# Softmax shares through the output bank, and weight pieces ordered behind matmuls, in a two-layer decoder kernel

## The chip, the cores and the metric

The kernel runs on one core of a Trainium2 chip. The metric is the device time of one execution in microseconds (us). A program for this core has five engines that run side by side, each with its own queue of instructions: TensorE (PE in the profile, with its weight loads as PEld), VectorE (DVE), ScalarE (ACT), GpSimd (POOL) and SyncE (SP, which here only issues DMAs).

## What is computed

The reference is a decoder of two layers on 512 tokens of width 1024, in fp32. Layer 0 is sparse attention beside memory attention and a squared-ReLU MLP. Then keys and values are computed once from the residual stream, and layer 1 reads them:

```python
k_s, v_s = jnp.split(rmsnorm(x, kv_norm) @ w_kv_shared, 2, axis=-1)
...
q, q_mem = jnp.split(h @ b_w_in[i], [B_Q], axis=-1)
o_main = dilated_attention(q, k_shared, v_shared, b_q_norm[i])
o_mem = memory_attention(q_mem, mem_kv, mem_q_norm[layer], mem_k_norm[layer])
x = x + jnp.concatenate([o_main, o_mem], axis=-1) @ b_w_out[i]
...
x = x + squared_relu_mlp(rmsnorm(x, mlp_norm[layer]), w_up[layer], w_down[layer])
```

The dilated attention of layer 1 has 8 heads and three groups of keys (window 128 at every position, 512 at every fourth, 2048 at every sixteenth). Each group has its own softmax, and the three outputs are added with weights that are a softmax over the groups' log-sums. The kernel calls these weights shares.

## The kernel before

Every matmul on fp32 data is made of three matmuls on split operands: a value is kept as a high part and the remainder (`mm3`, L234 to L239; lines 237, 238 and 239 are the three matmuls). A weight tile is loaded by SP into a staging buffer `st` (three buffers, `wdma`), and split into a tile `w` (four buffers) by one ACT and one DVE instruction.

Where the input of a projection went through a norm, the norm's gain is multiplied into the weights as they are split. `wload` then makes one piece per 128 rows of the contraction: `part` (L250) issues ACT L253 for the high part and DVE L254 for the remainder. Seven projections of layer B are of this kind: K and V (width 512), q of the four head pairs (width 384) and q of the memory attention (width 256). Each has eight contraction steps, so eight pieces.

`proj` (L277) runs a projection over four blocks of 128 tokens; a step is three matmuls for one of the eight pieces. During the first block (at steps 0, 2 and 4 with two steps per tile, at step 0 with four) it loads weight tiles so that two are ahead, and issues all pieces of a tile at once. The matmuls of the q projections go to two accumulator banks `s_acc`. A finished block is evacuated by `normf` (ACT L474, DVE L476 to L483) and DVE L1431, and some steps later its heads are transposed on PE (L677) into a bank of `s_pt` and copied out by ACT (L683, L1439).

PSUM has eight banks: two `s_acc`, three `s_ps` (scores), two `s_pt` (transposes) and one `s_po` (outputs of P times V).

Layer B runs K's projection, then q's of pair 0 and V's, then the attention of four head pairs. `attend` issues the attention as items, and between items takes steps from a list of other work: q of pairs 1 to 3 with their keys, q and keys of the memory attention, and parts of the output projection. An item's `front` makes scores, their maximum (DVE L1521) and the exponentials (ACT L1531); its `back`, one item later, transposes the probabilities (L1551, L1560) and, at the end of a group, multiplies by V (`close0` L1573 and `close1` L1586, in `s_po`).

The shares of a pair are a side chain, one step per tick:

- `turned_b` takes the first group's maxima and sums, transposes them (L1602), copies them to a row with the tokens in another order (DVE L1604), transposes back (L1608) and copies (DVE L1610).
- `shares_b` makes the shares from both groups' maxima and sums in small DVE operations (L1618 to L1630), splits them, transposes them (L1637), copies the rows (DVE L1641), and spreads them over the 64 columns of each head by a matmul each for the two groups: L1645, copied by ACT L1647, and L1649, multiplied into the first output by DVE L1650. `join_b` does the same for the second output and adds.

All five bank uses of this chain are in `s_pt`.

The text of the program is not the order on the engines. The program is built with

```python
with tile.TileContext(nc, schedule_with_timeline_sim=True) as tc:
```

which plans each engine's queue from simulated times: among the instructions whose inputs are there in the simulation, the one earlier in the text goes first. On the chip the queues run in that order, and semaphores hold an instruction until its inputs and buffers are ready.

Of the kernel before, what the change touches and what calls it, by code (L numbers as in the profile page):

```python
# [11 lines left out]
AF = mybir.ActivationFunctionType  # L12
ALU = mybir.AluOpType
AX = mybir.AxisListType

P = 128
D = 1024
S = 512
NB = 4
KT = 8  # L20
# [14 lines left out]
def bcast(ap, dim, n):  # L35

    a = [list(x) for x in ap.ap]
    a.insert(dim, [0, n])
    return bass.AP(tensor=ap.tensor, offset=ap.offset, ap=a)
# [13 lines left out]

WK = 0.4
DELAY = 5

NY, NZ = 1, 1
END, WAIT = object(), object()
# [106 lines left out]
class K:  # L165
# [46 lines left out]
        self.nc.sync.dma_start(st, src)  # L212
        return st

    def wload(self, src, lo="v", gains=None):

        st = self.wdma(src)
        w = self.t("w", [P, 2, src.shape[-1]], F32R)
        if gains is None:
            self.wsplit(w, st, lo)  # L220
            return w
        n = src.shape[-1] // gains.shape[1]
        for j in range(gains.shape[1]):
            c = slice(j * n, (j + 1) * n)
            self.part(w[:, :, c], st[:, c], gains[:, j : j + 1])
        return w

    def wsplit(self, w, st, lo):
# [5 lines left out]
    def mm3(self, ps, lh, rh, start, stop, again=False):  # L234

        mm = self.nc.tensor.matmul
        mm(ps, lh[0], rh[0], start=start, stop=False, skip_group_check=again)  # L237
        mm(ps, lh[0], rh[1], start=False, stop=False, skip_group_check=again)  # L238
        mm(ps, lh[1], rh[0], start=False, stop=stop, skip_group_check=again)  # L239

    def gcol(self, gname):

# [7 lines left out]
    def part(self, dst, src, g):  # L250

        nc = self.nc
        nc.scalar.activation(dst[:, 0], src, AF.Copy, scale=g)  # L253
        nc.vector.scalar_tensor_tensor(  # L254
            out=dst[:, 1], in0=src, scalar=g, in1=dst[:, 0], op0=ALU.mult, op1=ALU.subtract
        )

    def xg(self, x, gname):

# [17 lines left out]
    def proj(self, xg, wsrc, n, evac, blocks=NB, per=2, stat=None, banks=None, pool=None, lo="v", fine=False, hook=None, order=None, gain=None):  # L277


        ws = []  # L280
        if not stat:
            stat = lambda k, b: [xg[k][:, h, b * P : (b + 1) * P] for h in (0, 1)]

        def step(ps, k, b):
            w = ws[k // per]
            o = (k % per) * n
            self.mm3(ps, stat(k, b), [w[:, h, o : o + n] for h in (0, 1)], k == 0, k == KT - 1)

        late = []

        def tick(n=DELAY):
            for x in list(late):
                x[0] += 1
                if x[0] >= n:
                    late.remove(x)
                    x[1]()

        def out(b, ps):
            f = evac(b, ps)
            if f:  # L300
                late.append([0, f])

        if banks:
            banks = [self.ps(p, [P, n]) for p in banks]
            for k in range(KT):
                if hook:
                    hook(k)
                o = (k % per) * n
                if k % per == 0 and fine:
                    st = self.staged.pop(0) if self.staged else self.wdma(wsrc[k // per])  # L310
                    ws.append(self.t("w", [P, 2, per * n], F32R))
                elif k % per == 0:
                    ws.append(self.wload(wsrc[k // per], lo[len(ws) % len(lo)]))
                w = ws[-1]
                if fine:
                    self.wsplit(w[:, :, o : o + n], st[:, o : o + n], lo[k % len(lo)])
                for b in range(blocks):
                    self.mm3(banks[b], stat(k, b), [w[:, h, o : o + n] for h in (0, 1)], k == 0, k == KT - 1)
                yield
            for b in range(blocks):  # L320
                out(b, banks[b])
                yield
                tick(1)
        nw = KT // per
        order = order or range(blocks)
        for b in [] if banks else order:
            ps = None
            for k in range(KT):
                if b == order[0]:
                    while len(ws) < min(nw, k // per + 2):  # L330
                        i = len(ws) * per
                        gs = self.gcol(gain)[:, i : i + per] if gain else None
                        ws.append(self.wload(wsrc[len(ws)], lo[len(ws) % len(lo)], gs))
                if ps is None:
                    ps = self.ps(pool[b] if isinstance(pool, list) else pool or self.pacc, [P, n])
                step(ps, k, b)
                yield
                tick()
            out(b, ps)
            yield  # L340
        while late:
            tick()
            yield
# [1134 lines left out]
    def attn_b(self, sp, q4, kv, oT, side):  # L1478

        nc = self.nc  # L1480
        st0 = self.t("stt", [P, NB, 4])
        st1 = self.t("stt", [P, NB, 4])
        t0, t1 = {}, {}

        def front(s, w, ih):

            kp4 = kv[0]
            st = (st0, st1)[w]
            sizes = [P, 256] if w == 0 and ih == 0 else [256, 256]
            Sp = self.ps(self.pS, [P, sum(sizes)])  # L1490
            o = 0
            for ii in range(2):
                i, n = 2 * ih + ii, sizes[ii]
                blk = slice(i * P, (i + 1) * P)
                if w == 0:
                    for hl in (0, 1):
                        k = kp4[hl][:, s, (i + 1) * 32 - n // 4 :]
                        k = bass.AP(
                            tensor=k.tensor, offset=k.offset, ap=[list(k.ap[0]), [32, n // P], [P, 4], [1, 32]]
                        )  # L1500
                        nc.tensor.matmul(
                            Sp[:, o : o + n].rearrange("p (j r u) -> p j r u", r=4, u=32), q4[0][:, s, blk], k,
                            start=ii == 0 and hl == 0, stop=False,
                        )
                    nc.tensor.matmul(Sp[:, o : o + n], self.idb, self.bm0[:, 256 - n :], start=False, stop=ii == 1)
                else:
                    for g in range(2):
                        for hl in (0, 1):
                            nc.tensor.matmul(
                                Sp[:, o + g * P : o + g * P + P], q4[1 + g][:, s, blk], kp4[hl][:, s, blk],  # L1510
                                start=ii == 0 and g == 0 and hl == 0, stop=False,
# [25 lines left out]
                pg = p.rearrange("p (r g k) -> p r g k", r=2, g=2)  # L1537
                nc.gpsimd.tensor_tensor(out=pg[:, :, 0, :], in0=pg[:, :, 0, :], in1=pg[:, :, 1, :], op=ALU.add)
            if s == 1 and ih == 1:
                side.add(self.shares_b(st1, s0, acc) if w else self.turned_b(st0, s0))  # L1540
            return p

        def back(s, w, ih, p):
# [18 lines left out]
            if s == 1 and ih == 1:  # L1562
                close1()

        acc, s0 = [], []

        def close0():
            vn = kv[1]
# [25 lines left out]
        order = [(s, w, ih) for w in range(2) for s in range(2) for ih in range(2)]  # L1594
        return [Item(front, back, a, sp, sp or None) for a in order]

    def turned_b(self, st0, res):

        nc = self.nc
        pt = self.ps(self.pT, [4, S])  # L1600
        for b in range(NB):
            nc.tensor.transpose(pt[:, b * P : (b + 1) * P], st0[:, b, :], self.idf)  # L1602
        row = self.t("p2", [4, S])
        nc.vector.tensor_copy(row.rearrange("p (r u) -> p r u", r=4), self.perm(pt))  # L1604
        yield
        pt = self.ps(self.pT, [P, NB, 4])
        for r_ in range(NB):
            nc.tensor.transpose(pt[:, r_, :], row[:, r_ * P : (r_ + 1) * P], self.idf[0:4, 0:4])  # L1608
        s0 = self.t("stt", [P, NB, 4])
        nc.vector.tensor_copy(s0, pt)  # L1610
        res.append(s0)

    def shares_b(self, st1, s0, acc):

        nc = self.nc
        s0 = s0[0]
        m = self.t("nb", [P, NB, 2])
        nc.vector.tensor_tensor(out=m, in0=s0[:, :, 0:2], in1=st1[:, :, 0:2], op=ALU.min)  # L1618
        ee = self.t("nb", [P, 2, NB, 2])
        nc.vector.tensor_tensor(out=ee[:, 0], in0=m, in1=s0[:, :, 0:2], op=ALU.subtract)  # L1620
        nc.vector.tensor_tensor(out=ee[:, 1], in0=m, in1=st1[:, :, 0:2], op=ALU.subtract)
        nc.scalar.activation(ee, ee, AF.Exp)
        z = self.t("nb", [P, 2, NB, 2])
        nc.vector.tensor_tensor(out=z[:, 0], in0=ee[:, 0], in1=s0[:, :, 2:4], op=ALU.mult)
        nc.vector.tensor_tensor(out=z[:, 1], in0=ee[:, 1], in1=st1[:, :, 2:4], op=ALU.mult)
        nc.vector.tensor_tensor(out=m, in0=z[:, 0], in1=z[:, 1], op=ALU.add)
        nc.vector.reciprocal(out=m, in_=m)
        cc = self.t("nb", [P, NB, 2, 2])
        for w_ in range(2):
            nc.vector.tensor_tensor(out=cc[:, :, w_, :], in0=ee[:, w_], in1=m, op=ALU.mult)  # L1630
        ch = self.t("nb", [P, NB, 2, 4], F32R)
        self.split(ch.rearrange("p r t c -> p t r c"), cc.rearrange("p r w s -> p r (w s)"), "v")
        for _ in range(NY):
            yield
        pt = self.ps(self.pT, [8, S])
        for r_ in range(NB):
            nc.tensor.transpose(  # L1637
                pt[:, r_ * P : (r_ + 1) * P].bitcast(F32R), ch[:, r_].rearrange("p t c -> p (t c)"), self.idr
            )
        rows = self.t("p2", [8, S], F32R)  # L1640
        nc.vector.tensor_copy(rows, pt)  # L1641
        for _ in range(NZ):
            yield
        pc = self.ps(self.pT, [P, S])
        nc.tensor.matmul(pc, self.sel[:, 1, :], rows, start=True, stop=True)  # L1645
        cb = self.t("p2", [P, S])
        nc.scalar.activation(cb, pc, AF.Copy)  # L1647
        pc = self.ps(self.pT, [P, S])
        nc.tensor.matmul(pc, self.sel[:, 0, :], rows, start=True, stop=True)  # L1649
        nc.vector.tensor_tensor(out=acc[0], in0=acc[0], in1=pc, op=ALU.mult)  # L1650
        acc.append(cb)
# [135 lines left out]
```

## Time and profile before

| | |
|---|---|
| median of 3 runs | 1300.62 us (1298.31 to 1304.62) |
| the profiled execution's own time | 1302.66 us |
| its span, first to last instruction | 1300.6 us |
| mean granted TensorE clock | 0.990 |

In a profile's timeline a line has the start and the length in us, the engine, the line of the kernel, the operation, the output and inputs by tile name, shapes, a count, and in brackets the idle time of the engine before it and what ended that. An entry with a count is several instructions merged. In the waits, a line names the waiting engine and line, what it waited for, and the total us, the number of waits and the longest. Starts are counted from the span's start. Layer B before its MLP lies between about 675 and 960 us; the first weight piece of K's projection (ACT L253) starts at 677.2 us, and the last one, of the memory attention's q, at 842.7 us.

### The profile page before, as it was taken

Reading aid. Unit: us, or ns where it says so; the run is one execution under the profiler, and the core shown is the slowest. Engines: PE = TensorE matmul, PEld = TensorE weight load, DVE = VectorE, ACT = ScalarE, POOL = GpSimd, SP = SyncE. Lnnn points to the kernel's source line nnn. Section 1 sums busy time; section 2 is a strip of 40 time slices with the busy share of each in tenths; the row PEclk is TensorE's granted clock in tenths of the full one; section 3 lists DMA queues with packets and bytes.
Section 4 is the critical chain, followed back from the end, with each engine's and each line's share of the span. In section 5 each row is a group of like instructions: output and inputs, shape, how many; then the busy total and the mean of one; then the engine's idle time right before and its main releaser. Section 6 shows DMA issues by size and latency. Waiting matters only on the chain.

```text
span 1300.6 us, 18592 instructions
## 1 busy us (share of the span) xinstructions
PE 1252.5 (96%) x6425; PEld 1017.7 (78%) x6425; DVE 987.0 (76%) x1687; ACT 765.6 (59%) x1763; POOL 540.1 (42%) x569
## 2 busy tenths in 40 slices
PE   8998999999999999999999998899899999999998
PEld 6776776677787888888878897787678788888886
DVE  5978777764679678696799678776658968779678
ACT  5757667773555464554566576776666545455452
POOL 3766565532164241441425946442316424144241
PEclk9999999999999999999999999999899999999999
DMA  8222211023423425335254242002242442623423
GB/s 304 96 73 100 66 36 55 18 66 124 139 86 120 140 97 170 121 96 164 82 149 146 78 129 75 25 26 76 86 135 83 137 138 82 194 98 119 145 93 114
DMA packets 52686, 139.11 MB, mean 107 GB/s; under 512 B 5776, under 2 KB 14992, under 8 KB 52592
## 3 DMA queue, kind: packets, MB, share of 16 engines
q1 hardware_dynamic: 51376, 134.66, 32.9%
q0 software_dynamic: 640, 2.21, 0.5%
q8 instruction: 51, 0.84, 0.2%
q10 hardware_dynamic: 576, 1.05, 0.2%
q14 instruction: 43, 0.35, 0.1%
HBM read 132.66 MB, written 5.24 MB: 106 GB/s over the span
## 4 chain that ended last, share of the span: by engine, by line
PE 59%; DVE 24%; ACT 10%; DMA 3%; issue 2%; POOL 2%; ACTq 0%; POOLq 0%; DVEq 0%
PE s_ps L238 10%; PE s_ps L239 10%; PE s_ps L237 10%; DVE s_w L232 7%; PE s_acc L237 4%; PE s_acc L238 4%; PE s_acc L239 4%; DVE s_p L1114 2%; PE s_po L1055 2%; PE s_pt L238 2%; PE s_pt L239 2%; PE s_pt L237 2%; ACT s_w L230 2%; DVE s_w L254 2%; DVE s_qk L275 2%
## 5 line engine op out<-in xcount | busy, mean ns | idle before, releaser
L232 DVE TENSOR_TENSOR s_w<-s_st,s_w 128x1024 fp32r<-128x1024 f32 (+4 forms) x155 | 183.9, 1188 | 138.3 <-ACT s_w L230 138.0
L230 ACT ACTIVATE s_w<-s_st 128x1024 fp32r<-128x1024 f32 (+4 forms) x182 | 166.0, 917 | 137.9 <-PE s_pt L239 39.5
L237 PE MATMUL s_ps<-s_act,s_w 128*128 128x512 f32 x592 | 231.8, 393 | 3.2 <-ACT s_act L272 1.4
L238 PE MATMUL s_ps<-s_act,s_w 128*128 128x512 f32 x592 | 231.0, 390 | 0.0
L239 PE MATMUL s_ps<-s_act,s_w 128*128 128x512 f32 x592 | 230.9, 391 | 0.0
L1100 POOL TENSOR_TENSOR s_x<-s_x,s_st 128x512 f32<-128x512 f32 x64 | 106.0, 1679 | 91.0 <-DVE s_w L232 91.0
L237 PEld LDWEIGHTS s_ps<-s_act,s_w 128*128 128x128 f32 x592 | 110.9, 188 | 28.0 <-ACT s_act L272 3.2
L239 PEld LDWEIGHTS s_ps<-s_act,s_w 128*128 128x128 f32 x592 | 111.2, 188 | 22.9
L238 PEld LDWEIGHTS s_ps<-s_act,s_w 128*128 128x128 f32 x592 | 111.2, 188 | 22.8 <-DVE s_act L275 0.4
L237 PE MATMUL s_acc<-s_w,s_act 128*128 128x512 f32 (+2 forms) x304 | 112.0, 374 | 9.8 <-ACT s_w L230 6.0
L1100 POOL TENSOR_TENSOR s_x<-s_qki,s_st 128x512 f32<-128x512 f32 x16 | 25.5, 1596 | 216.2 <-DMA s_st<-in_w_db_dram 196.6
L238 PE MATMUL s_acc<-s_w,s_act 128*128 128x512 f32 (+2 forms) x304 | 111.6, 368 | 1.4 <-DVE s_w L232 0.9
L239 PE MATMUL s_acc<-s_w,s_act 128*128 128x512 f32 (+2 forms) x304 | 109.4, 364 | 0.0
L652 POOL TENSOR_SCALAR s_p<-s_p,s_cr 128x256 f32<-128x256 f32 (+3 forms) x128 | 70.9, 568 | 68.3 <-DVE s_cr L1018 20.2
L232 DVE TENSOR_TENSOR s_w<-s_x,s_w 128x512 fp32r<-128x512 f32 x96 | 89.3, 971 | 4.9 <-ACT s_w L230 4.9
L275 DVE TENSOR_TENSOR s_qk<-s_p,s_qk 128x256 fp32r<-128x256 f32 (+1 forms) x96 | 83.9, 886 | 2.8 <-ACT s_qk L272 1.8
L230 ACT ACTIVATE s_w<-s_x 128x512 fp32r<-128x512 f32 x96 | 56.8, 624 | 41.0 <-POOL s_x L1100 41.0
L232 POOL TENSOR_TENSOR s_w<-s_st,s_w 128x512 fp32r<-128x512 f32 (+4 forms) x27 | 39.0, 1443 | 87.0 <-ACT s_w L230 84.3
L272 ACT ACTIVATE s_qk<-s_p 128x256 fp32r<-128x256 f32 (+1 forms) x96 | 47.0, 489 | 45.4 <-DVE s_p L1228 43.2
L237 PEld LDWEIGHTS s_acc<-s_w,s_act 128*128 128x128 f32 x304 | 58.7, 195 | 16.6 <-ACT s_w L230 6.2
L238 PEld LDWEIGHTS s_acc<-s_w,s_act 128*128 128x128 f32 x304 | 59.3, 195 | 7.8 <-DVE s_w L232 1.8
L1222 ACT ACTIVATE s_p<-s_ps 128x512 f32<-128x512 f32 x64 | 37.8, 591 | 46.1 <-PE s_ps L239 43.8
(357 smaller groups left out, 3223.6 us busy)
## 6 DMA issues: line engine op xcount, KB each, us to landing
s_st<-in_w_db_dram SPq DMA_DIRECT2D x80, 512.0 KB, 3.6
s_st<-in_w_up_dram SPq DMA_DIRECT2D x64, 512.0 KB, 3.8
s_st<-in_w_bq_dram SPq DMA_DIRECT2D x16, 384.0 KB, 3.3
s_st<-in_w_ag_dram SPq DMA_DIRECT2D x11, 512.0 KB, 4.3
s_act<-in_w_c_dram SPq DMA_DIRECT2D x8, 512.0 KB, 5.4
s_st<-in_w_mem_dram SPq DMA_DIRECT2D x8, 512.0 KB, 3.6
s_st<-in_w_ao_dram SPq DMA_DIRECT2D x16, 256.0 KB, 2.7
s_tq<-in_w_db_dram SPq DMA_DIRECT2D x16, 256.0 KB, 3.1
```

The lines of the kernel that those rows point to most:

```text
L230: nc.scalar.activation(w[:, 0], st, AF.Copy)
L232: self.low = e.tensor_tensor(out=w[:, 1], in0=st, in1=w[:, 0], op=ALU.subtract)
L237: mm(ps, lh[0], rh[0], start=start, stop=False, skip_group_check=again)
L238: mm(ps, lh[0], rh[1], start=False, stop=False, skip_group_check=again)
L239: mm(ps, lh[1], rh[0], start=False, stop=stop, skip_group_check=again)
L254: nc.vector.scalar_tensor_tensor(out=dst[:, 1], in0=src, scalar=g, in1=dst[:, 0], op0=ALU.mult, op1=ALU.subtract)
L272: nc.scalar.activation(dst[:, 0], src, AF.Copy)
L275: nc.vector.tensor_tensor(out=dst[:, 1], in0=src, in1=dst[:, 0], op=ALU.subtract)
L652: self.nc.gpsimd.tensor_scalar(out=p, in0=p, scalar1=c, scalar2=1.0, op0=ALU.mult, op1=ALU.mult)
L1055: nc.tensor.matmul(O[x * 64 : x * 64 + 64, q0 + o : q0 + 256], v[:, j, br, :], st[x][br][:, j, o:256], start=half == 0 and br == 1 and j = ...
L1100: self.nc.gpsimd.tensor_tensor(out=o, in0=x, in1=b[:, i * 512 : (i + 1) * 512], op=ALU.add)
L1222: nc.scalar.activation(u, ps, AF.Relu)
```

## The change

Two things are changed.

The shares' chain takes its five banks per pair from `s_po` (pool `pO`, one bank) in place of `s_pt` (pool `pT`, two banks). Its statistics of both groups now lie in one tile, so that three pairs of small DVE operations become one operation each.

In `proj`, pieces with a gain are not issued as soon as their tile is loaded. They are kept in a list, and at step k of the first block as many are issued as bring the number made to k + 3. From step 1 on each of the two instructions of a piece gets an edge to the last matmul issued so far. The edge has the class `NoSync`: it orders the planning and adds no semaphore.

```diff
+AHEAD = 3
+DEPC, DEPR = mybir.DependencyClass.NoSync, mybir.DependencyReason.DATA
...
-    def wload(self, src, lo="v", gains=None):
+    def wload(self, src, lo="v", gains=None, late=None):
...
-            self.part(w[:, :, c], st[:, c], gains[:, j : j + 1])
+            f = lambda c=c, j=j: self.part(w[:, :, c], st[:, c], gains[:, j : j + 1])
+            if late is None:
+                f()
+            else:
+                late.append(f)
...
-        mm(ps, lh[1], rh[0], start=False, stop=stop, skip_group_check=again)
+        self.last = mm(ps, lh[1], rh[0], start=False, stop=stop, skip_group_check=again)
...
-                        ws.append(self.wload(wsrc[len(ws)], lo[len(ws) % len(lo)], gs))
+                        ws.append(self.wload(wsrc[len(ws)], lo[len(ws) % len(lo)], gs, parts))
+                    while parts and made < min(KT, k + AHEAD):
+                        f = parts.pop(0)
+                        for x in f():
+                            if k:
+                                self.tc.add_manual_dep(x.ins, self.last.ins.name, mybir.DependencyInfo(DEPC, DEPR), reason="late split")
+                        made += 1
...
-        st1 = self.t("stt", [P, NB, 4])
+        sb = self.t("stt", [P, 2, NB, 4])
+        st1 = sb[:, 1]
...
-        pt = self.ps(self.pT, [4, S])
+        pt = self.ps(self.pO, [4, S])
...
-        pt = self.ps(self.pT, [P, NB, 4])
+        pt = self.ps(self.pO, [P, NB, 4])
...
-        nc.vector.tensor_tensor(out=ee[:, 0], in0=m, in1=s0[:, :, 0:2], op=ALU.subtract)
-        nc.vector.tensor_tensor(out=ee[:, 1], in0=m, in1=st1[:, :, 0:2], op=ALU.subtract)
+        tt(ee, bcast(m, 1, 2), sb[:, :, :, 0:2], ALU.subtract)
...
-        nc.vector.tensor_tensor(out=z[:, 0], in0=ee[:, 0], in1=s0[:, :, 2:4], op=ALU.mult)
-        nc.vector.tensor_tensor(out=z[:, 1], in0=ee[:, 1], in1=st1[:, :, 2:4], op=ALU.mult)
+        tt(z, ee, sb[:, :, :, 2:4], ALU.mult)
...
-        for w_ in range(2):
-            nc.vector.tensor_tensor(out=cc[:, :, w_, :], in0=ee[:, w_], in1=m, op=ALU.mult)
+        tt(cc.rearrange("p r w s -> p w r s"), ee, bcast(m, 1, 2), ALU.mult)
...
-        pt = self.ps(self.pT, [8, S])
+        pt = self.ps(self.pO, [8, S])
...
-        pc = self.ps(self.pT, [P, S])
+        pc = self.ps(self.pO, [P, S])
...
-        pc = self.ps(self.pT, [P, S])
+        pc = self.ps(self.pO, [P, S])
```

More of the change, by code (lines that the diff above doesn't have):

```diff
@@ L252, in part @@
         nc = self.nc
[L253 to L256, printed above, removed]
+        return [
+            nc.scalar.activation(dst[:, 0], src, AF.Copy, scale=g),
+            nc.vector.scalar_tensor_tensor(
+                out=dst[:, 1], in0=src, scalar=g, in1=dst[:, 0], op0=ALU.mult, op1=ALU.subtract
+            ),
+        ]
     def xg(self, x, gname):
@@ L323, in proj @@
                 tick(1)
-        nw = KT // per
+        nw, parts, made = KT // per, [], 0
         order = order or range(blocks)
@@ L1539, in front @@
             if s == 1 and ih == 1:
-                side.add(self.shares_b(st1, s0, acc) if w else self.turned_b(st0, s0))
+                side.add(self.shares_b(sb, acc) if w else self.turned_b(st0, sb[:, 0]))
             return p
@@ L1563, in back @@
                 close1()
-        acc, s0 = [], []
+        acc = []
         def close0():
@@ L1595, in attn_b, with turned_b @@
         return [Item(front, back, a, sp, sp or None) for a in order]
-    def turned_b(self, st0, res):
+    def turned_b(self, st0, s0):
         nc = self.nc
-        pt = self.ps(self.pT, [4, S])
+        pt = self.ps(self.pO, [4, S])
         for b in range(NB):
@@ L1605, in turned_b, with shares_b @@
         yield
-        pt = self.ps(self.pT, [P, NB, 4])
+        pt = self.ps(self.pO, [P, NB, 4])
         for r_ in range(NB):
             nc.tensor.transpose(pt[:, r_, :], row[:, r_ * P : (r_ + 1) * P], self.idf[0:4, 0:4])
-        s0 = self.t("stt", [P, NB, 4])
         nc.vector.tensor_copy(s0, pt)
-        res.append(s0)
-    def shares_b(self, st1, s0, acc):
+    def shares_b(self, sb, acc):
         nc = self.nc
-        s0 = s0[0]
+        tt = lambda o, x, y, op: nc.vector.tensor_tensor(out=o, in0=x, in1=y, op=op)
         m = self.t("nb", [P, NB, 2])
-        nc.vector.tensor_tensor(out=m, in0=s0[:, :, 0:2], in1=st1[:, :, 0:2], op=ALU.min)
+        tt(m, sb[:, 0, :, 0:2], sb[:, 1, :, 0:2], ALU.min)
         ee = self.t("nb", [P, 2, NB, 2])
-        nc.vector.tensor_tensor(out=ee[:, 0], in0=m, in1=s0[:, :, 0:2], op=ALU.subtract)
-        nc.vector.tensor_tensor(out=ee[:, 1], in0=m, in1=st1[:, :, 0:2], op=ALU.subtract)
+        tt(ee, bcast(m, 1, 2), sb[:, :, :, 0:2], ALU.subtract)
         nc.scalar.activation(ee, ee, AF.Exp)
         z = self.t("nb", [P, 2, NB, 2])
-        nc.vector.tensor_tensor(out=z[:, 0], in0=ee[:, 0], in1=s0[:, :, 2:4], op=ALU.mult)
-        nc.vector.tensor_tensor(out=z[:, 1], in0=ee[:, 1], in1=st1[:, :, 2:4], op=ALU.mult)
-        nc.vector.tensor_tensor(out=m, in0=z[:, 0], in1=z[:, 1], op=ALU.add)
+        tt(z, ee, sb[:, :, :, 2:4], ALU.mult)
+        tt(m, z[:, 0], z[:, 1], ALU.add)
         nc.vector.reciprocal(out=m, in_=m)
         cc = self.t("nb", [P, NB, 2, 2])
-        for w_ in range(2):
-            nc.vector.tensor_tensor(out=cc[:, :, w_, :], in0=ee[:, w_], in1=m, op=ALU.mult)
+        tt(cc.rearrange("p r w s -> p w r s"), ee, bcast(m, 1, 2), ALU.mult)
         ch = self.t("nb", [P, NB, 2, 4], F32R)
```

## The prediction

> **What bounds the kernel now.** The page comes first, for the engine that sets the time.
>
> ```profile
> PE 1252.5 (96%) x6425; PEld 1017.7 (78%) x6425; DVE 987.0 (76%) x1687; ACT 765.6 (59%) x1763; POOL 540.1 (42%) x569
> ```
>
> TensorE is busy for 1252.5 of 1300.6 us, so idle PE time in the whole program is 48.1 us, and no edit that leaves the matmuls as they are can win more than that plus what a slow clock costs. The change touches only layer B before its MLP, so the next view is the busy time by stretch there, chosen in pairs: a stretch at half clock, and the one just ahead of it. The columns are the stretch, its length, busy us (instructions) of PE, PEld, DVE, ACT and POOL, the granted clock, the DMA share, GB/s.
>
> ```profile
> 799.80:806.40 6.60, 4.66 (x30) 3.99 (x29) 6.57 (x12) 6.10 (x17) 3.38 (x4) 1.00 0.49 132
> 806.50:809.90 3.40, 3.40 (x13) 3.40 (x12) 3.40 (x5) 2.21 (x7) 3.19 (x4) 0.50 0.40 161
> 843.90:847.30 3.40, 1.36 (x13) 1.20 (x13) 2.99 (x9) 2.35 (x9) 1.55 (x2) 1.00 0.66 180
> 847.40:850.80 3.40, 3.40 (x19) 3.40 (x18) 3.37 (x8) 2.17 (x8) 3.17 (x5) 0.51 0.16 46
> 915.00:919.00 4.00, 2.60 (x15) 1.61 (x13) 3.02 (x6) 1.37 (x5) 0.45 (x1) 1.00 0.57 144
> 919.20:929.30 10.10, 9.79 (x40) 7.46 (x40) 5.64 (x11) 6.86 (x23) 2.50 (x5) 0.50 0.30 92
> ```
>
> Three times PE is poorly filled (4.66 of 6.60, 1.36 of 3.40, 2.60 of 4.00 us) and then runs at half clock though it is full. Matmul work done at 0.50 takes twice as long, so the half-clock stretches cost about 1.7, 1.7 and 5.0 us. Next, what PE waited for in that stage, from the waits of PE between 650 and 940 us (total, times, longest).
>
> ```profile
> PE s_pt L677 <- DVE s_p L1641: 1.5, 1, 1.5
> PE s_pt L1637 <- ACT s_qk L1439: 1.4, 1, 1.4
> PE s_pt L1645 <- ACT s_qk L635: 1.4, 1, 1.4
> ...
> PE s_acc L237 <- DVE s_tq L1431: 1.1, 1, 1.1
> ...
> PE s_acc L238 <- DVE s_w L254: 0.5, 1, 0.5
> ```
>
> The first three are waits for a bank of the transposes' pool, s_pt: the shares (L1637, L1645) wait for one, or q's transposes (L677) wait for the bank that the shares hold until L1641 has copied it. The fourth is a projection that waits for its accumulator. Only the last is a matmul that waits for a weight piece. Then the timelines show why these were late. PE, then ACT, then DVE:
>
> ```profile
> 843.52 0.41 PE L1637 MATMUL s_pt<-idr,s_nb 128*8 128x128 f32 x4 [1.38 <-ACT s_qk L1439]
> 845.38 0.70 PE L677 MATMUL s_pt<-idr,s_qki 128*128 128x128 f32 x6 [1.46 <-DVE s_p L1641]
> ```
>
> ```profile
> 841.51 1.69 ACT L253 ACTIVATE s_w<-s_st,gv 128x256 fp32r<-128x256 f32 x4
> 843.10 0.36 ACT L1439 ACTIVATE s_qk<-s_pt 128x256 fp32r<-128x256 f32 x1
> ```
>
> ```profile
> 841.19 3.54 DVE L254 SCALAR_TENSOR_TENSOR s_w<-s_st,gv,s_w 128x256 fp32r<-128x256 f32 x8
> 844.66 0.67 DVE L1641 CAST s_p<-s_pt 8x512 fp32r<-8x512 f32 x1
> ```
>
> L1439, which would empty a bank, stands on ACT behind four weight pieces; L1641, which would empty the other, stands on DVE behind all eight. The accumulator's wait has the same form, here on DVE and on PE:
>
> ```profile
> 799.77 4.54 DVE L254 SCALAR_TENSOR_TENSOR s_w<-s_st,gv,s_w 128x384 fp32r<-128x384 f32 x6
> ...
> 804.81 0.56 DVE L1431 TENSOR_TENSOR s_tq<-s_acc,gr 128x384 f32<-128x384 f32 x1
> ```
>
> ```profile
> 805.42 0.44 PE L237 MATMUL s_acc<-s_w,s_act 128*128 128x384 f32 x1 [1.05 <-DVE s_tq L1431]
> ```
>
> Six pieces run in a block, the evacuation L1431 comes after them, and PE starts 0.05 us after it ends. So two things meet in this stage: the shares take banks that transposes need, and pieces for the next projection, made in one block, hold up the evacuations that free banks.
>
> **Part 1, the shares through the O bank.** Five bank uses per head pair leave s_pt (two banks) for s_po (one, which until now holds the two P times V outputs). Out of the sum go the three s_pt waits: 1.5 + 1.4 + 1.4 = 4.3 us. New is that in one bank each use must be emptied before the next. Three of these waits are there already as data (rows copied before the next transposes, and so on). Two are new: the second share product L1649 waits for the copy L1647 of the first, and the second P times V, L1586, waits for the product L1650. PE, ACT and DVE of one pair:
>
> ```profile
> 816.09 0.49 PE L1645 MATMUL s_pt<-s_p,s_ab 8*128 8x512 f32 x1
> ...
> 818.27 0.49 PE L1649 MATMUL s_pt<-s_p,s_ab 8*128 8x512 f32 x1
> ...
> 820.84 0.55 PE L1586 MATMUL s_po<-s_pt,s_x 128*64 128x128 f32 x6 [0.31 <-ACT s_pt L660]
> ```
>
> ```profile
> 816.61 0.60 ACT L1647 ACTIVATE s_p<-s_pt 128x512 f32<-128x512 f32 x1 [0.70 <-PE s_pt L1645]
> ```
>
> ```profile
> 818.80 0.69 DVE L1650 TENSOR_TENSOR s_raw<-s_raw,s_pt 128x512 f32<-128x512 f32 x1 [0.76 <-PE s_pt L1649]
> ```
>
> The copy ends at 817.21, 1.06 us before L1649 begins; the product ends at 819.49, 1.35 us before L1586 begins. Both new waits would have been over here, so I cost them at nothing; matmuls of the projection and the next pair's scores lie between them and are the cover. Without cover each pair pays the copy and the product, 0.60 + 0.69, or 5.2 us over four pairs. Behind a waiting L1649 or L1586 in PE's queue stand exactly those matmuls.
>
> **Part 2, the shares' smaller form.** Three of the small DVE operations per pair go, twelve in all, of about this size (from the groups of lines):
>
> ```profile
> L1630 DVE TENSOR_TENSOR s_nb<-s_nb,s_nb 128x8 f32<-128x8 f32 x8 | 2.3, 325 | 0.1
> ```
>
> That is some 12 x 0.325 = 3.9 us of DVE time. Each joined one is twice as long in elements, so the gain may be near nothing. On PE's path I count 0: by the rows above, the shares' end is not what L1586 waits for.
>
> **Part 3, the pieces.** Seven projections (K, V, four of q, mem q) make eight pieces each, one ACT and one DVE instruction per piece. The first three stay free; piece j of the other five is queued behind the last matmul of step j - 3 (or of other work, if that stands later in the text). No instruction is added. Moved past them on ACT and DVE are the evacuations (L1439, L1641, L1431), and that takes out the 1.1 us of the accumulator, and with the shares' banks gone from s_pt also what would be late next: with L1637 elsewhere, L677 would still have waited for L1439 behind the four ACT pieces. The loads on SP keep their order, but a staging buffer comes free when its last piece is made, so the next load, and the loads behind it in SP's queue, may start later. Five pieces of 0.83 us (row below) bound that at 4.1 us per projection; the load is issued a tile ahead of its use, which covers it, and I count 0.
>
> Against that, pieces come closer to their use. Their pace on DVE, from the groups by shape between 700 and 930 us (count, then busy us and mean ns):
>
> ```profile
> L254 DVE SCALAR_TENSOR_TENSOR s_w<-s_st,gv,s_w 128x384 fp32r<-128x384 f32 x32 | 25.0, 827 | 4.2 <-ACT s_w L253 4.2
> ...
> L254 DVE SCALAR_TENSOR_TENSOR s_w<-s_st,gv,s_w 128x512 fp32r<-128x512 f32 x8 | 9.0, 1174 | 0.0
> ```
>
> And the pace at which a block uses them, two starts nine matmuls, or three steps, apart:
>
> ```profile
> 799.18 0.33 PE L237 MATMUL s_acc<-s_w,s_act 128*128 128x384 f32 x1
> ...
> 800.74 0.33 PE L237 MATMUL s_acc<-s_w,s_act 128*128 128x384 f32 x1
> ```
>
> A step of width 384 takes 1.56 / 3 = 0.52 us, so by width 0.69 for 512 and 0.35 for 256; a piece of 256 is by width 0.55. PE can outrun DVE by 0.31, 0.48 or 0.20 us per ordered piece. Five pieces: 4 x 5 x 0.31 + 2 x 5 x 0.48 + 5 x 0.20 = 12.0 us if nothing else fills PE, and 0 if scores and transposes do. The nearest row is V's first block, whose pieces are the slow ones of 1.174 us and are used almost as made: it shows a PE wait of 0.5 us. I take that for V and the three q projections inside attention: 2.0 us.
>
> **The clock.** The two half-clock stretches at 806.5 and 847.4 follow the very stretches whose waits go, so I take off 1.7 + 1.7. Ahead of the third, one of two waits goes (the 1.4 of L1645); I take one 3.4 us part of its three as gone, 1.7. The Trainium skill, "TensorE: Matmul & The Clock Gate", in "Why this matters for your kernels", asks only that PE not be idle for more than about 3 us between bursts. The longest of the waits quoted is 1.46 us and the clock halved all the same, so the measurement decides against that rule; by it this term would be zero, and the time that of the first rival.
>
> **The sum.** Waits gone: 4.3 + 1.1 = 5.4. Clock: 5.1. Back again: 2.0 for pieces, and 1.4 because I expect one of the three bank waits to be replaced by another. -5.4 - 5.1 + 2.0 + 1.4 = -7.1 us. The profiled execution took 1302.66 us (span 1300.6), so it would take 1295.6; it lies 2.0 above the median of the runs, 1300.62, inside their spread of 1298.31 to 1304.62. On the median the forecast is 1293.5.
>
> **Rivals.**
>
> *The clock stays.* What comes before a slow stretch is not only waits but transposes (L677, L1462, L1637), and those stay. The same page, in "Part 4: PE-mode transpose", says that transposes do not count as busy in the way matmuls do. If they are what halves the clock, only the waits go: -5.4 + 3.4 = -2.0, or 1298.6, no change. For it: the 1.36 of 3.40 before 847.4 is almost all transposes. Against it: the waits are there in all three run-ups too, and no row here shows the one without the other. Chance 0.15.
>
> *The order does not hold the pieces apart.* The edges shape the queues when they are planned; no semaphore is added. If the planner issues the matmuls early, or ACT and DVE fall behind it, pieces run in a block as before. Then the accumulator's 1.1 and L1439's wait stay, and only about 1.5 us of bank waits goes: 1299.1, no change. Chance 0.10.
>
> *The first blocks starve, and it is slower.* DVE is busy for 6.57 of 6.60 us before 806.4, so late pieces compete with the evacuations that they used to delay. If nothing fills PE, the 12.0 us are paid, and each of the four first blocks inside attention is a poorly filled stretch that brings its own 1.7 us at half clock, 6.8. With the forecast's gains kept: 12.0 + 6.8 - 5.4 - 5.1 = +8.3, or 1308.9. It becomes slower by over 0.5% when more than about 10 of the 12.0 us stay uncovered. For it: just-in-time work gives up what was made early. Against it: 0.5 us of such waits where the pieces are slowest. Chance 0.20.
>
> **How the numbers follow.** Half a per cent, 6.5 us, is about what a measurement of this kernel can tell from no change: faster is below 1294.1, slower above 1307.1. The forecast has 0.55, its own range is 1287 (all 8.4 us of slow clock gone, nothing back: -13.8) to 1298, and the point lies just inside faster; I put 0.43 of it there and 0.12 in no change. No change gets 0.12 + 0.15 + 0.10 = 0.37, slower 0.20, faster 0.43. The range for 8 in 10 leaves out half of the slow case above 1309 and the best tenth below 1285.
>
> **What would show it.** Right: up to about 660 us the two traces agree; L1637, L1645 and L1649 write s_po; the three s_pt waits are gone; L254 comes in runs of one to three; fewer stretches at 0.50 between 800 and 930 us; DVE has twelve fewer instructions. Wrong: PE waits for L253 or L254 of more than 2 us, waits of s_po matmuls for L1647 or L1650, or new half-clock stretches at the start of a projection.

## The result, and the profile after

The changed kernel takes 1287.72 us (median of 6 runs, 1286.79 to 1289.21) where the kernel before takes 1300.51 (6 runs): a ratio of 0.9903, 95% interval 0.9887 to 0.9918, so 12.8 us less. The profiled execution took 1286.79 us, with a span of 1285.0 and a mean granted clock of 0.999. Later, beside the last experiments, the same kernel gave 0.9895 (0.9878 to 0.9911).

Lines of the code have moved: the three matmuls are L243 to L245 in the kernel after, a piece is ACT L260 and DVE L261, the evacuation L1431 is L1445, the copies L1439 are L1453, q's transposes L677 are L691, and the shares' L1637, L1645 and L1649 are L1647, L1655 and L1659.

The first view cuts the program at marks that both kernels have: the first piece of K's projection, the last piece of the memory attention's q, and the last gain-scaled activation of the MLP behind layer B. The columns are those of the prediction's stretches. The kernel before, then the kernel after:

```profile
677.20:746.00 68.80, 67.06 (x335) 57.52 (x334) 56.65 (x118) 41.51 (x115) 45.49 (x61) 1.00 0.39 127
746.00:842.70 96.70, 91.14 (x609) 83.20 (x607) 73.35 (x145) 69.88 (x217) 50.42 (x62) 0.98 0.25 74
842.70:962.80 120.10, 108.97 (x687) 86.08 (x688) 81.93 (x180) 85.00 (x256) 35.68 (x52) 0.94 0.25 76
```

```profile
674.70:744.00 69.30, 68.91 (x342) 58.79 (x341) 57.46 (x118) 41.32 (x117) 45.96 (x63) 1.00 0.40 126
744.00:839.40 95.40, 92.36 (x634) 84.49 (x634) 74.36 (x148) 72.42 (x230) 54.66 (x65) 1.00 0.26 76
839.40:947.40 108.00, 100.51 (x663) 79.92 (x662) 76.83 (x164) 79.88 (x243) 34.02 (x48) 0.98 0.28 84
```

Layer B takes 272.7 us in place of 285.6, 12.9 us less, as much as the whole change of the medians. Most of it (12.1) lies in the last stretch. PE's idle time, length less busy time, falls from 18.4 to 10.9 us (-7.5), and its busy time from 267.2 to 261.8 (-5.4) although it does the same matmuls: that part is the clock, 0.94 and 0.98 before in the later stretches, 0.98 and 1.00 after. All runs together say the same. A run's time multiplied by its mean granted clock is an estimate of what it would take without half clock, since PE is nearly always busy in the half-clock stretches of the kernel before (3.40 of 3.40 and 9.79 of 10.10 us). The kernel before has 57 runs beside the experiments and the kernel after has 10 in all: by their means this estimate falls from 1289.7 to 1281.9 us (-7.8), and the rest of the time, the clock's part, from 10.9 to 5.5 us (-5.4). The MLP behind takes 337.8 and 337.6 us. Ahead of layer B the profiled execution of after gains 2.5 us (677.2 to 674.7). There the queues of PE, DVE, ACT and POOL have the same order in both traces. The trace of before has 10.2 us at half clock there and that of after none, and such stretches come and go between runs.

The waits of PE between 670 and 960 us come to 17.7 us before and 9.5 after. The first of them after:

```profile
PE s_acc L244 <- DVE s_w L261: 3.7, 5, 1.7
PE s_acc L243 <- DVE s_x L1108: 1.5, 1, 1.5
PE s_ps L601 <- ACT s_p L660: 1.1, 1, 1.1
```

No wait for a share's bank is left, and none of an accumulator for L1445. The longest sum is now matmuls that wait for a weight piece, 3.7 us in five waits, where there was one of 0.5. Two of them stand in the first block of the memory attention's q:

```profile
838.07 0.39 PE L244 MATMUL s_acc<-s_w,s_act 128*128 128x256 f32 x1 [0.63 <-DVE s_w L261]
...
841.87 0.58 PE L244 MATMUL s_acc<-s_w,s_act 128*128 128x256 f32 x1 [1.70 <-DVE s_w L261]
```

```profile
838.30:841.70 3.40, 1.75 (x12) 1.31 (x11) 3.20 (x7) 3.30 (x11) 2.97 (x4) 1.00 0.44 115
841.70:845.10 3.40, 3.23 (x16) 3.24 (x17) 3.40 (x8) 1.95 (x6) 2.59 (x3) 0.50 0.29 78
```

This is the one half-clock stretch that layer B has left in this trace, and it has the form of the three before: PE filled for 1.75 of 3.40 us, then half clock. In sum layer B spent 17.0 us at half clock before and 3.4 after.

### The profile page after: what moved, and what is told of

Same layout as the page of the kernel before. It is cut to its first block, busy times and chain, and to the rows that moved or that the text cites. A ratio compares the mean times of both kernels' runs of the same rounds, so it can differ in the third digit from the quotient of the medians.

```text
span 1285.0 us, 18569 instructions
## 1 busy us (share of the span) xinstructions
PE 1241.8 (97%) x6425; PEld 1009.8 (79%) x6425; DVE 981.1 (76%) x1675; ACT 762.4 (59%) x1763; POOL 543.0 (42%) x569
## 4 chain that ended last, share of the span: by engine, by line
PE 66%; DVE 20%; ACT 7%; DMA 3%; issue 2%; POOL 1%; ACTq 0%; DVEq 0%; POOLq 0%
PE s_ps L244 11%; PE s_ps L245 10%; PE s_ps L243 10%; DVE s_w L238 7%; PE s_acc L244 5%; PE s_acc L243 5%; PE s_acc L245 5%; PE s_pt L244 3%; PE s_pt L245 3%; PE s_pt L243 3%; DVE s_p L1128 2%; PE s_po L1069 2%; ACT s_w L236 2%; DVE s_qk L283 2%; PE s_acc L834 1%
## 5 line engine op out<-in xcount | busy, mean ns | idle before, releaser
L243 PE MATMUL s_ps<-s_act,s_w 128*128 128x512 f32 x592 | 231.7, 393 | 1.9 <-ACT s_act L280 1.4
L245 PE MATMUL s_ps<-s_act,s_w 128*128 128x512 f32 x592 | 230.8, 390 | 0.0
L243 PEld LDWEIGHTS s_ps<-s_act,s_w 128*128 128x128 f32 x592 | 111.0, 188 | 26.8 <-ACT s_act L280 3.2
L245 PEld LDWEIGHTS s_ps<-s_act,s_w 128*128 128x128 f32 x592 | 111.2, 188 | 22.9
L243 PE MATMUL s_acc<-s_w,s_act 128*128 128x512 f32 (+2 forms) x304 | 110.6, 369 | 6.9 <-ACT s_w L236 6.1
L245 PE MATMUL s_acc<-s_w,s_act 128*128 128x512 f32 (+2 forms) x304 | 108.2, 360 | 0.0
L243 PEld LDWEIGHTS s_acc<-s_w,s_act 128*128 128x128 f32 x304 | 58.0, 192 | 13.6 <-ACT s_w L236 6.3
L244 PEld LDWEIGHTS s_acc<-s_w,s_act 128*128 128x128 f32 x304 | 58.3, 192 | 12.8 <-DVE s_w L261 6.2
```

Of the source, the lines that this page charges most:

```text
L245: self.last = mm(ps, lh[1], rh[0], start=False, stop=stop, skip_group_check=again)
```

## The experiments

Three explanations stood against each other. A: shares and pieces each remove waits of their own, and both count. B: only the pieces matter, since the banks were late because evacuations stood behind pieces. C: any new order of the queues moves the time by some microseconds, whatever it is meant for. All ratios are to the kernel before, run on the same chip (medians there 1299.81 to 1301.05 us), with 95% intervals.

**The shares alone.** The whole change of the shares; pieces are issued at once.

```diff
-ws.append(self.wload(wsrc[len(ws)], lo[len(ws) % len(lo)], gs, parts))
+ws.append(self.wload(wsrc[len(ws)], lo[len(ws) % len(lo)], gs))
```

> The shares through the O bank with their smaller form; all weight pieces of a tile issued at once, as in the kernel before. Theory A (the two parts work on two different waits and add up): the three bank waits of the shares go, and with them most of the half-clock stretches at 847 and 919 us, so about half of the gain: 1300.5 - 6, near 1294 to 1295; waits of an accumulator for L1431's counterpart behind a block of pieces stay. Theory B (only the pieces matter, since the banks were late because of the evacuations queued behind pieces): within 2 us of 1300.5. Theory C (any new order of the queues gives some gain or loss of this size): no relation to the parts; this and the kernel with the pieces alone need not add up to 12.8.

Measured: 1292.18 us (9 runs, 1286.76 to 1296.4), ratio 0.9934 (0.9913 to 0.9956). B is out: more than half of the gain is there without touching a piece. What the pieces were to remove is still in its waits, and larger than before the change:

```profile
PE s_acc L243 <- DVE s_tq L1445: 2.7, 2, 1.9
PE s_acc L244 <- DVE s_w L261: 1.5, 4, 0.5
```

**The pieces alone.** `attn_b`, `turned_b` and `shares_b` as in the kernel before, all else as after.

> The pieces held back and ordered behind matmuls; the shares as in the kernel before (in the transposes' banks, larger form). Theory A: the accumulator's wait of 1.1 us and the half-clock stretch at 806 us go, 4 to 5 us of PE waits for pieces come, so 1295 to 1297, with the shares' bank waits still in the waits of PE. Theory B: nearly the whole gain, 1288 to 1290, without waits for the shares' banks. Theory C: anything from 1285 to 1305 that does not add up with the shares alone.

Measured: 1299.41 us (12 runs), ratio 0.9992 (0.9979 to 1.0006). Nothing that can be told from no change, and slower than theory A expected. The accumulator's wait for L1445 is gone here too, and waits for pieces came in its place. A also expected the shares' bank waits to stay, and most of them went: the waits of a share for a bank, and of other matmuls for a bank that a share held, come to 5.2 us in the trace before and to 1.6 here. So the order of the pieces frees those banks, as B says, but that is not where the time is. The waits of all matmuls that write s_pt are 8.7 us before, 4.5 here and 1.0 after the whole change:

```profile
PE s_acc L244 <- DVE s_w L261: 4.0, 5, 1.4
PE s_acc L243 <- ACT s_w L236: 1.3, 1, 1.3
PE s_pt L1476 <- ACT s_qk L1453: 1.1, 3, 0.4
PE s_pt L691 <- ACT s_pt L674: 1.1, 2, 0.8
...
PE s_pt L1565 <- DVE s_raw L1664: 0.5, 1, 0.5
...
PE s_pt L1651 <- ACT s_pt L674: 0.4, 1, 0.4
```

(L1651 makes the shares' transposes here, and L1664 is the product that frees a share's bank.)

**The pieces' place in the text without the edges.**

```diff
-                            if k:
+                            if False:
```

> The changed kernel with the pieces in the same places of the text but without the edges to the matmuls. If the edges do the work (the planner takes a piece as soon as its load has landed, whatever its place in the text), the time is that of the shares alone, about 1294, and pieces run in blocks of four to eight again. If the place in the text is enough, the time is that of the changed kernel, 1287.7 within 1.5.

Measured: 1293.59 us (9 runs), ratio 0.996 (0.9941 to 0.9979). In the traces its queues of PE, DVE, ACT and POOL have the same operations on the same tiles in the same order as the kernel with the shares alone. So the place in the text does nothing, and the edges make the whole difference. It is also a measure of the method: two programs with the same queues on those four engines gave 0.9934 and 0.996, so differences under about 0.3% are not read here.

**Five pieces ahead for the narrow projection.**

```diff
-                    while parts and made < min(KT, k + AHEAD):
+                    while parts and made < min(KT, k + (AHEAD if n > 256 else 5)):
```

> The changed kernel with five pieces ahead in place of three for the memory attention's q alone (steps of width 256, 0.35 us). In the changed kernel its first block waits 0.6 and 1.7 us for pieces and is followed by the one half-clock stretch that is left. If that starving is the cause of the stretch: waits for pieces fall from 3.7 us to about 1.5, the stretch goes, and the time falls by 2 to 4 us, to 1284 to 1286. If the half clock comes from the transposes there, the waits go and the stretch stays: 1285.5 to 1287. If a block of pieces comes back with five ahead: no gain or a loss of 1 to 3 us.

Measured: 1290.14 us (6 runs), ratio 0.993 (0.9909 to 0.9951). Waits for pieces fell to 1.4 us, and the half-clock stretch at 842 us was not in its trace. No gain came of it: another stretch stood at 908 us, and there are new waits of scores for keys. Nor does it show that the starving caused the stretch at 842 us. A second trace of the changed kernel, with the same queues and 3.8 us of waits for pieces, has no half clock there either and has its one stretch at 906 us. The time fits the third case, and five of this projection's pieces stand in a row on DVE, but 0.993 against 0.9903 is under 0.3%.

```profile
PE s_ps L1516 <- DVE s_qk L647: 1.6, 2, 1.2
PE s_acc L243 <- DVE s_x L1108: 1.5, 1, 1.5
PE s_acc L244 <- DVE s_w L261: 1.4, 3, 0.9
```

**Two and five pieces ahead everywhere.**

```diff
-AHEAD = 3
+AHEAD = 2
```

> The changed kernel with two pieces ahead in place of three: pieces 2 to 7 are ordered behind the step two before their use. If nearness to the use starves PE (the slower rival's mechanism), waits of matmuls for pieces rise from 3.7 us to 8 or more and the time goes up by 4 to 10 us, to 1292 to 1298. If scores and transposes fill PE anyway, the time stays within 2 us of the changed kernel.

Measured: 1288.32 us (6 runs), ratio 0.9906 (0.9887 to 0.9926), with only 1.1 us of waits for pieces. The second kernel has `AHEAD = 5`:

> The changed kernel with five pieces ahead in all seven projections: only pieces 5 to 7 are ordered. If spreading the pieces is what the edges give, much of it is lost: runs of five pieces on ACT and DVE, and a time between the changed kernel (1287.7) and the kernel with the shares alone (1292 to 1294). If three was near starving, it is as fast or faster, 1285 to 1288, with under 2 us of waits for pieces.

Measured: 1288.77 us (6 runs), ratio 0.9911 (0.9886 to 0.9935), 2.2 us of waits for pieces. Both expectations of a change failed. Between two and five, how near a piece is to its use makes no difference that these runs can show, and nearer did not mean more starving.

**The shares through the scores' banks.** In `turned_b` and `shares_b`, `self.pO` is replaced by `self.pS`.

> The changed kernel with the shares through the scores' banks (three, s_ps) in place of the output's bank (one, s_po). If what counts is that the shares leave the transposes' banks, the time is near the changed kernel's, 1287 to 1291. If the scores now wait for a bank that a share holds while ACT or DVE is late, waits of s_ps matmuls for share copies appear and the time is 1293 or more. If the one s_po bank costs anything by its order, this is faster than 1287.

Measured: 1291.05 us (6 runs), ratio 0.9925 (0.9905 to 0.9945). Most of the gain is there with other banks, so it comes from leaving the transposes' banks. The new waits that could have come, of scores for share copies, are not among its larger ones. The opposite ones are: the shares' first transposes (L1617) wait for a bank that a score holds until its exponentials (L1546) are made.

```profile
PE s_ps L1617 <- ACT s_p L1546: 1.1, 5, 0.4
```

**The smaller form alone.** Pieces at once, and in `turned_b` and `shares_b` `self.pO` replaced by `self.pT`.

> The kernel before with the smaller form of the shares alone (twelve DVE operations fewer), the shares in the transposes' banks and the pieces issued at once. If the small operations are off the path, as the forecast counts: within 1.5 us of the kernel before. If the shares' end is on the path: 2 to 4 us faster.

Measured: 1306.12 us (12 runs, 1300.67 to 1307.1), ratio 1.0028 (1.0011 to 1.0044). Twelve instructions fewer, and if anything slower. Its profiled execution has 20.4 us at half clock in layer B and 3.6 us of accumulators' waits for L1445. The queues of layer B stand in another order than before, beyond the instructions that are left out. That this order cost more than the instructions saved is C's explanation; it is argued here, not shown.

**The smaller form with ordered pieces.** As after, with `self.pT` in the shares.

> The smaller form of the shares in the transposes' banks, with the pieces ordered behind matmuls: the changed kernel with its bank change undone. So far (ratio to the kernel before): smaller form alone 1.0028, with the O bank 0.9934 and 0.996, with O bank and ordered pieces 0.9903. If the bank carries the gain: 1300 or above here. If the ordered pieces repair what the smaller form alone lost: 1295 to 1299.

Measured: 1298.59 us (12 runs), ratio 0.9986 (0.9973 to 0.9999). The time lies in the second case. Without the bank change the other two parts together are worth 1 to 2 us, which is under 0.3%.

**The larger form, with O bank and ordered pieces.** `turned_b` and `shares_b` of before with `self.pO`.

> The changed kernel with the larger form of the shares (twelve small DVE operations more), O bank and ordered pieces kept. If the smaller form is worth nothing by itself: within 2 us of the changed kernel. If its 3.9 us of DVE time count once the banks are out of the way: 2 to 4 us slower. If every new order of the queues moves the time by some us whatever it is for: 3 us or more away on either side, with no wait in the trace that names the small operations.

Measured: 1289.95 us (6 runs), ratio 0.9918 (0.9903 to 0.9933). The changed kernel gave 1286.46 us on the same chip, 3.5 us less, but its ratio of 0.9895 (0.9878 to 0.9911) has an interval that overlaps with this one. The cases are not decided by it.

**The bank alone.** The same, with pieces issued at once.

> Nothing but the bank change: the shares in the O bank in their larger form, pieces issued at once. If the bank carries most of the gain: 1291 to 1294, as with the smaller form. If the two kernels with the smaller form and the O bank owed it to the form: 1298 or more.

Measured: 1291.0 us (5 runs), ratio 0.9927 (0.9913 to 0.994). One name changed in five places gives 9.0 us of the change's 12.8. Its first wait shows what the pieces were aimed at:

```profile
PE s_acc L243 <- DVE s_tq L1445: 2.6, 3, 1.2
PE s_ps L601 <- ACT s_p L660: 1.6, 1, 1.6
```

**The changed kernel again**, beside the last three:

> The changed kernel again, beside the three above on one chip: 1286 to 1290. Its half-clock stretches should change from run to run ahead of layer B, where its queues are those of the kernel before, and so spread the runs by 2 to 3 us.

Measured: 1286.46 us (4 runs, 1286.15 to 1287.8), ratio 0.9895 (0.9878 to 0.9911). No kernel tried is faster by more than these runs can tell. The expected spread between runs did not show in these four; it did in the nine of the shares alone.

All eight combinations of the three parts are then measured:

| | larger form | smaller form |
|---|---|---|
| transposes' banks, pieces at once | 1 (before) | 1.0028 |
| transposes' banks, pieces ordered | 0.9992 | 0.9986 |
| O bank, pieces at once | 0.9927 | 0.9934 and 0.996 |
| O bank, pieces ordered | 0.9918 | 0.9903 and 0.9895 (after) |

Down each column the O bank takes off 0.7% to 0.9%, whichever form and pieces go with it, and the scores' banks did nearly the same. For the bank this rules C out, as far as one order of the queues in each kernel can. The pieces' order takes off 0.1% with the larger form and 0.3% to 0.7% with the smaller one. The smaller form's own differences, up to 0.3% either way, are too small to be read from the times alone.

The runs can be split by the clock as in the section on the result. Each cell has the mean time without half clock plus the clock's part, in us (standard errors 0.2 to 0.7 and 0.4 to 0.9):

| | larger form | smaller form |
|---|---|---|
| transposes' banks, pieces at once | 1289.7 + 10.9 (before) | 1292.7 + 12.1 |
| transposes' banks, pieces ordered | 1288.1 + 11.0 | 1288.5 + 9.9 |
| O bank, pieces at once | 1285.5 + 5.4 | 1284.5 + 8.4 |
| O bank, pieces ordered | 1282.0 + 7.7 | 1281.9 + 5.5 (after) |

The two programs with the same queues, 1284.8 + 7.0 and 1284.3 + 9.8, differ in the clock's part alone. The O bank takes 4.2 to 8.2 us off the first term and 3.3 to 5.5 us off the second. The ordered pieces take 1.6 to 4.2 us off the first, with the larger form too. The clock's part moves with them by +0.1 and +2.3 us in the larger form, and by -2.2 and -2.9 us in the smaller. The smaller form adds 3.0 us to the first term in the transposes' banks with pieces at once, and changes it by 1.0 us or less in the other three pairs.

## Why the prediction was right, point by point

**The direction and the bound.** The gain lies where the prediction put it, in layer B before its MLP, in PE's idle time and its clock. The forecast was -7.1 us and the measured change is -12.8, within the range but only 0.7 us from its fast end. That end stood for all 8.4 us of slow clock gone and no wait back. What came was less from the clock (5.4) and more from waits (7.5), so it is in part luck that the total stayed inside.

**Part 1, the shares' bank.** Right that the shares in the transposes' banks cost time. The three bank waits of 4.3 us are gone, the bank alone has most of the gain (0.9927), and the scores' banks do nearly the same (0.9925). The two new waits that were costed at nothing cost nothing: no matmul on s_po waits for L1657's copy or L1660's product in the trace after. But these three waits are not what the gain consists of, since the ordered pieces alone, in their trace, removed most of them as well, and the time did not change by anything that can be told. With the two banks no longer held by a share, other users stopped waiting: the keys' transposes had this row among the waits of the kernel before (sum in us, number, longest), and have none after. The sum had only the shares' own waits.

```profile
PE s_pt L1462 <- ACT s_qk L1439: 1.9, 4, 0.6
```

**Part 2, the smaller form.** It was counted 0. By itself it is 0.3% slower, or 3.0 us without half clock; with ordered pieces and the O bank it makes no difference that can be told. The forecast left out that it reorders the queues.

**Part 3, the pieces.** The accumulator's wait of 1.1 us went as predicted, and pieces took its place: 3.7 us where 2.0 was added. Alone they are worth nothing that the time can tell (0.9992), and 1.6 us by the split. The mark that was given for being wrong, over 2 us of waits for pieces, was met while the kernel got faster: waits for pieces count only against what else is waited for. So was another mark: the half-clock stretch at 841.7 us begins in the first block of a projection. The runs of one to three pieces were wrong too. After has runs of five (V) and four (q of pair 3) on DVE, and all eight pieces of pair 1's q follow each other there with nothing between but waits for ACT:

```profile
721.04 5.85 DVE L261 SCALAR_TENSOR_TENSOR s_w<-s_st,gv,s_w 128x512 fp32r<-128x512 f32 x5
...
745.06 2.21 DVE L261 SCALAR_TENSOR_TENSOR s_w<-s_st,gv,s_w 128x384 fp32r<-128x384 f32 x4
747.89 1.14 DVE L261 SCALAR_TENSOR_TENSOR s_w<-s_st,gv,s_w 128x384 fp32r<-128x384 f32 x2 [0.63 <-ACT s_w L260]
749.98 1.15 DVE L261 SCALAR_TENSOR_TENSOR s_w<-s_st,gv,s_w 128x384 fp32r<-128x384 f32 x2 [0.94 <-ACT s_w L260]
...
794.67 4.28 DVE L261 SCALAR_TENSOR_TENSOR s_w<-s_st,gv,s_w 128x384 fp32r<-128x384 f32 x4
```

**The clock.** Forecast -5.1 us, measured -5.4 by PE's busy time and by all runs. By half the length of the stretches, which is how the forecast counted, it is 6.8 in this trace. The size agrees, the places do not, so the close agreement is luck: all three stretches went, the long one at 919 us whole where a third was counted, and one came at 841.7 us.

**What came back.** This is the term that was mis-sized. The sum added 1.4 us for a bank wait in place of another and 2.0 for pieces, so waits were to win 2.0 net. PE's idle time in layer B fell by 7.5, and the time without half clock by 7.8 over all runs. No bank wait came back. Instead the smaller s_pt waits that the sum did not list went as well: the waits of matmuls that write s_pt fell from 8.7 us to 1.0, where the sum had 4.3 gone and 1.4 back. Those of matmuls that write s_acc rose from 4.6 to 5.6, with the pieces.

**The rivals.** That the clock stays is refuted by the clock's 17.0 us of half speed that became 3.4, and by runs: the mean granted clock over all runs is 0.992 before (23 runs beside the shares alone) and 0.996 after. Starving first blocks exist (3.7 us) but do not grow when pieces come nearer (1.1 us with two ahead). The rival that the order does not hold the pieces apart was half right: runs of four to eight remain, and the spacing chosen makes no difference that the runs can show.

**What stays open.** Why the ordered pieces give 0.3% to 0.7% with the smaller form and 0.1% with the larger is not settled. By the split above they save waits with both, and the difference lies in the clock's part, which falls with the smaller form only. Why it does is not known. The sums of PE's waits in layer B with the O bank lie within 4 us (12.7 and 10.5 with pieces at once in the smaller form, 9.5 and 8.9 after), and no single wait accounts for it. That it is the order the planner happens to find is argued, not shown. Nor is the bank's gain traced in full: with the O bank the s_pt waits fall by 2.2 to 5.3 us from trace to trace, and the time without half clock by 4.2 to 8.2.

## What to carry to other kernels

When short side chains share a small pool of PSUM banks with the transposes that feed the main work, move the side chain to a bank that is seldom used, even if it is a single one. In the trace after, no step of the chain waits for another to leave that bank, and the waits on the pool that was left fell from 8.7 us to 3.4 with the bank alone and to 1.0 with the whole change. Cost such a move by all waits on that pool, not by the side chain's own. With a planner that orders queues by simulated times, measure each part alone and in pairs, because removing twelve instructions made the kernel slower and ordering the pieces showed a gain in the time only in company.

## What the runs showed of the hardware

Half clock follows a poorly filled stretch of about 3.4 us, with no idle gap near that length. This was counted in all 14 traces between 30 and 1270 us. The longest wait in the 3.4 us ahead of a half-clock stretch is 2.2 us. The stretches of one trace begin on a grid of 3.41 us and last one, two or three of its steps, and 5022 steps have full clock. Of the 4744 in which PE was busy for 80% or more, none was followed by half clock; of the 169 at 70% to 80% it was 4, of the 68 at 60% to 70% 24, and of the 41 below that 22. In the kernel with the smaller form alone the same pair appears at another place:

```profile
787.10:790.50 3.40, 1.41 (x11) 1.21 (x10) 2.75 (x6) 1.35 (x5) 1.90 (x3) 1.00 0.00 0
790.50:793.90 3.40, 3.40 (x12) 3.40 (x11) 2.37 (x5) 1.17 (x5) 3.11 (x5) 0.50 0.00 0
```

Transposes fill a stretch as matmuls do. In the kernel before, 21 of the 24 matmuls between 864.5 and 867.9 us are transposes (L1551, L677, L1602, L1608), and the other three take 0.8 us at most. PE is busy for 2.85 of 3.40 us, and the next stretch has full clock:

```profile
864.50:867.90 3.40, 2.85 (x24) 2.04 (x23) 3.31 (x8) 2.21 (x7) 0.00 (x0) 1.00 0.00 0
867.90:871.30 3.40, 3.08 (x28) 2.45 (x29) 1.38 (x3) 3.40 (x16) 1.86 (x3) 1.00 0.02 5
```

```profile
L1551 PE MATMUL s_pt<-c,s_p 128*128 128x128 f32 x7 | 1.2, 288 | 0.0
L677 PE MATMUL s_pt<-idr,s_qki 128*128 128x128 f32 x6 | 1.0, 278 | 0.0
L1602 PE MATMUL s_pt<-c,s_stt 128*4 128x128 f32 x4 | 0.6, 272 | 0.0
L1608 PE MATMUL s_pt<-c,s_p 4*128 4x4 f32 x4 | 0.4, 204 | 0.5 <-DVE s_p L1604 0.5
L1515 PE MATMUL s_ps<-bm,idb 128*128 128x512 bf16 x1 | 0.4, 390 | 0.0
L1509 PE MATMUL s_ps<-s_qk,s_qk 128*128 128x128 f32 x2 | 0.4, 274 | 0.0
```

The 14 traces have 44 steps in which PE is busy for 80% or more with its transposes and for less than half without them. None was followed by half clock. The Trainium skill, "TensorE: Matmul & The Clock Gate", says in "Part 4: PE-mode transpose" that transposes do not count as busy in the same way. These transposes, which are matmuls against an identity in fp32, did not lower the clock; whether they run in the mode that the section speaks of, the traces do not say.

Which poorly filled stretches are followed by half clock changes from run to run. The two traces of the changed kernel have the same queues, and their one half-clock stretch in layer B is at 841.7 us in the one and at 906.2 in the other. The nine runs of the shares alone spread from 1286.76 us at a mean clock of 1.000 to 1296.4 at 0.993.
